# One transformer layer on one core: V in 512-column matmuls, and an opening whose VectorE and ScalarE steps stand in one fixed order

## The chip, the core and the metric

The kernel runs on one core of a Trainium2 chip. Five engines matter: TensorE (PE in the profile, with its weight loads as PEld), VectorE (DVE), ScalarE (ACT), GpSimd (POOL) and SyncE (SP, which issues most DMAs). Each engine works through its own list of instructions in the order in which they were put there, and waits at semaphores for the others. The metric is the device time of one execution in microseconds (us): 1761.19 us is the median of three runs of the kernel before (1760.97 to 1761.48).

## The reference

One decoder layer over 1024 tokens of 1024 channels in float32, cut to what matters here:

```
h = rms_norm(x, attn_norm_w)
q, k, v, u, g = split(h @ w_in)         # 1024, 1024, 1024, 2048, 2048 columns
a = diff_attention(rms_norm(q), rms_norm(k), v, ...)   # 8 heads
c = causal_depthwise_conv(u_a * sigmoid(u_b), conv_w)  # width 31
c = silu(layer_norm(c))
x = x + (sigmoid(g_a) * (a @ w_pa) + sigmoid(g_b) * (c @ w_pc)) @ w_out
x = x + (silu(h2 @ w_g) * (h2 @ w_u)) @ w_down         # h2 = rms_norm(x)
```

The change touches the first line, the V columns of `w_in`, and the order in which the first steps are done. What is computed stays the same.

## The kernel before

**Every product in three.** Each float32 operand is split into a high part (a cast on ScalarE, `split_hi`, L119) and a low part (a subtraction on VectorE, `split_lo`, L124). A product of two operands is three matmuls, high by high, high by low and low by high, added up in one PSUM bank.

**Stages.** The first stage forms h, transposed and split as `hT_hi` and `hT_lo`, and from it V (stored to DRAM), the u blocks (U0 to U7, 128 channels each, with the gated product stored to DRAM) and the first head's q and k. Then comes attention, head by head, into whose gaps the other q, k and gate columns are worked. The projections, the output product and the feed-forward part follow. On VectorE the 248 multiply-adds of the convolution ("taps", L519 and L525, on 128x1024 tiles) run as a background list from the first u block to the end of attention; a fixed rate of 3.25 taps per item step is handed out in the first stage (`TAPS_FIRST`).

**The opening.** x comes in eight tiles of 128 tokens (`xt`). For each, ScalarE squares and sums it (L609), VectorE and ScalarE form the reciprocal root (L573 to L578, L603), VectorE multiplies two halves by it and by the norm's weights (L613, `xt<-xt,r,anw_b`), PE transposes eight 128x128 pieces into two PSUM tiles (L616, `px`, two buffers), ScalarE casts them to `hT_hi` and VectorE subtracts to `hT_lo`. The norm's weights are read from DRAM once for every partition (L173, 512 KB into `anw_b`).

**V and u.** V is four items of 256 columns (V0 to V3). An item's weights are two tiles of 128x1024 (`ld_wide`), and for every token tile 24 matmuls run with a 128x128 block of hT as the stationary operand and 256 weight columns as the moving one (L152 to L154, `pg<-whi,hT_hi`). A u item is two blocks of weights, each multiplied with the two halves of the tokens: the weights stand, 512 tokens move (`pg<-hT_hi,whi`), 24 matmuls for each half and block.

**What sets the order.** A scheduler puts the instructions on each engine by its own estimate of when each would be ready, unless `after(...)` holds a piece back behind a named instruction. The list of items (`first`) sets which come early: V0, U0, U1, V1 and so on. In the kernel before, nothing holds the opening's pieces in an order, and the scheduler interleaves norms, transposes and matmuls.

## Time and profile before

| what | value |
|---|---|
| median of three runs | 1761.19 us (1760.97 to 1761.48) |
| the profiled execution's own time | 1761.41 us |
| its span, first to last instruction | 1759.6 us |
| PE busy | 1740.3 us (99%) |
| weight loads, PEld | 1503.1 us (85%) |
| VectorE busy | 1273.2 us (72%) |
| ScalarE busy | 800.5 us (45%) |
| DMA, mean | 156 GB/s |

The profiled execution lies 0.2 us above the median; 1.8 us of its time lie outside the span. A matmul's duration in the trace runs from its start to the end of its drain, and the next one starts before that: the rate is read from start to start. "Idle before" an instruction is put down to the engine or DMA whose semaphore came last.

### The profile page before, as it was taken

What the parts mean: (1) busy time and instruction counts of PE and PEld (TensorE: products, weight loads), DVE (VectorE), ACT (ScalarE), POOL (GpSimd) and SP (SyncE); (2) the same over time, 40 slices, a digit from 0 to 9 for tenths busy, and PEclk for the clock granted to TensorE, in tenths of its full rate; (3) what the DMA queues carried; (4) which work ended last, traced back from release to release, by engine and by line L of the source; (5) the groups of instructions that cost most, each with busy time, mean ns of one, the idle gap of its engine ahead of it and who ended that gap; (6) DMA issues with size and microseconds to landing.
All of it is one profiled execution on the core that took longest, in us unless ns stands there. A gap on an engine that the chain in (4) does not pass through costs nothing.

```text
span 1759.6 us, 25844 instructions
## 1 busy us (share of the span) xinstructions
PE 1740.3 (99%) x9367; PEld 1503.1 (85%) x9367; DVE 1273.2 (72%) x2187; ACT 800.5 (45%) x1886; POOL 26.7 (2%) x106
## 2 busy tenths in 40 slices
PE   7999999999999999999999999999999999999999
PEld 6898998988999998988888888888888888888887
DVE  6388879999988888886687534877667666664544
ACT  4211241558767776655557313643333333333332
POOL 3000000000000000000000000000000000000000
PEclk9999999999999999999999999999999999999999
DMA  8433353235444344352983544234544544697663
GB/s 248 164 121 114 108 158 124 76 96 151 111 138 124 88 114 138 86 163 76 336 268 108 168 167 144 91 102 146 177 150 158 176 157 139 210 360 242 215 216 131
DMA packets 255728, 275.34 MB, mean 156 GB/s; under 512 B 16064, under 2 KB 177896, under 8 KB 255600
## 3 DMA queue, kind: packets, MB, share of 16 engines
q1 hardware_dynamic: 253568, 267.45, 47.6%
q0 software_dynamic: 1744, 5.19, 1.0%
q8 instruction: 74, 1.21, 0.3%
q10 hardware_dynamic: 288, 1.05, 0.2%
q14 instruction: 54, 0.44, 0.1%
HBM read 176.59 MB, written 78.68 MB: 145 GB/s over the span
## 4 chain that ended last, share of the span: by engine, by line
PE 95%; DMA 2%; ACT 1%; DVE 1%; issue 0%; SPq 0%; ACTq 0%
PE acc L1375 22%; PE pg L153 15%; PE pg L154 15%; PE pg L152 15%; PE acc L451 12%; PE sc L817 2%; PE sc L816 2%; PE wo L154 2%; PE wo L153 2%; PE wo L152 2%; PE pT L852 2%; PE pW L152 1%; PE pW L154 1%; PE pW L153 1%; PE pQ L714 1%; DMA wraw<-in_w_in_dram 1%
## 5 line engine op out<-in xcount | busy, mean ns | idle before, releaser
L525 DVE SCALAR_TENSOR_TENSOR acc<-u,cw,acc 128x1024 f32<-128x1024 f32 x240 | 306.8, 1278 | 2.8
L152 PE MATMUL pg<-whi,hT_hi 128*128 128x256 f32 x768 | 220.3, 287 | 1.2 <-ACT hT_hi L119 1.2
L154 PE MATMUL pg<-whi,hT_lo 128*128 128x256 f32 x768 | 219.8, 286 | 0.4 <-DVE hT_lo L124 0.4
L153 PE MATMUL pg<-wlo,hT_hi 128*128 128x256 f32 x768 | 219.1, 285 | 0.2 <-DVE wlo L124 0.2
L119 ACT CAST whi<-wraw 128x1024 fp32r<-128x1024 f32 x109 | 114.4, 1051 | 215.9 <-PE pg L153 122.1
L152 PE MATMUL pg<-hT_hi,whi 128*128 128x512 f32 x512 | 201.6, 394 | 0.0
L154 PE MATMUL pg<-hT_hi,wlo 128*128 128x512 f32 x512 | 200.9, 393 | 0.0
L153 PE MATMUL pg<-hT_lo,whi 128*128 128x512 f32 x512 | 200.5, 392 | 0.0
L124 DVE TENSOR_TENSOR wlo<-wraw,whi 128x1024 fp32r<-128x1024 f32 x109 | 132.8, 1219 | 70.8 <-ACT whi L119 66.7
L124 DVE TENSOR_TENSOR wlo<-draw,whi 128x1024 fp32r<-128x1024 f32 x75 | 91.8, 1224 | 89.6 <-ACT whi L119 84.3
L152 PEld LDWEIGHTS pg<-whi,hT_hi 128*128 128x128 f32 x768 | 147.7, 192 | 4.2 <-ACT hT_hi L119 2.5
L154 PEld LDWEIGHTS pg<-whi,hT_lo 128*128 128x128 f32 x768 | 147.8, 192 | 2.3 <-DVE hT_lo L124 1.1
L153 PEld LDWEIGHTS pg<-wlo,hT_hi 128*128 128x128 f32 x768 | 147.7, 192 | 2.0 <-DVE wlo L124 0.5
L119 ACT CAST whi<-draw 128x1024 fp32r<-128x1024 f32 x75 | 79.1, 1055 | 129.5 <-PE acc L451 125.9
L451 PE MATMUL acc<-wlo,whi 128*128 128x512 f32 x308 | 119.8, 389 | 0.0
L451 PE MATMUL acc<-whi,wlo 128*128 128x512 f32 x308 | 119.8, 389 | 0.0
L823 ACT ACTIVATE E<-E,mn 128x256 f32<-128x256 f32 (+7 forms) x128 | 99.7, 779 | 35.8 <-DVE mn L818 33.6
L154 PEld LDWEIGHTS pg<-hT_hi,wlo 128*128 128x128 f32 x512 | 96.2, 188 | 19.0
L153 PEld LDWEIGHTS pg<-hT_lo,whi 128*128 128x128 f32 x512 | 96.2, 188 | 18.7
L152 PEld LDWEIGHTS pg<-hT_hi,whi 128*128 128x128 f32 x512 | 96.3, 188 | 18.3
L1375 PE MATMUL acc<-h_hi,whi 128*128 128x512 f32 x240 | 93.4, 389 | 0.0
L1375 PE MATMUL acc<-h_lo,whi 128*128 128x512 f32 x240 | 93.4, 389 | 0.0
(270 smaller groups left out, 3951.5 us busy)
## 6 DMA issues: line engine op xcount, KB each, us to landing
wraw<-in_w_gate_up_dram SPq DMA_DIRECT2D x44, 512.0 KB, 4.8
wraw<-in_w_in_dram SPq DMA_DIRECT2D x40, 512.0 KB, 4.5
qs<-qs SPq DMA_DIRECT2D x96, 128.0 KB, 2.3
wd<-in_w_down_dram SPq DMA_DIRECT2D x44, 256.0 KB, 3.1
tdT<-wd SPq DMA_DIRECT2D x88, 128.0 KB, 4.3
draw<-sdS SPq DMA_DIRECT2D x44, 256.0 KB, 3.8
draw<-tdT SPq DMA_DIRECT2D x44, 256.0 KB, 3.9
wraw<-in_w_in_dram SPq DMA_DIRECT2D x32, 256.0 KB, 3.3
```

The costliest lines, as they stand in the source:

```text
L119: act.copy(dst, src)
L124: last_lo[0] = dve.tensor_tensor(dst, src, f32(hi), op=ALU.subtract).ins
L152: pe.matmul(o, lh, rh, start=start, stop=False)
L153: pe.matmul(o, lh, rl, start=False, stop=False)
L154: last_mm[0] = pe.matmul(o, ll, rh, start=False, stop=stop).ins
L451: m = pe.matmul(o[s_][i][:], l_[:, ts], r_[:, 512:], start=start and j + y_ == 0, stop=j == n - 1 and y_ == 2, skip_group_check=not start,)
L525: dve.scalar_tensor_tensor(acc[0][:], us[c][:, t : t + S], cw[:, c, t : t + 1], acc[0][:], op0=ALU.mult, op1=ALU.add)
L816: pe.matmul(o[:, :w], qh[:, qs], k, start=True, stop=False)
L817: last_mm[0] = pe.matmul(o[:, :w], ql[:, qs], k, start=False, stop=True).ins
L823: act.activation(e[:, :nk], e[:, :nk], AF.Exp, bias=mn[:, j : j + 1], scale=-1.0, accum_out=l[:, j : j + 1])
L852: pe.transpose(pt[:, k * P : (k + 1) * P], e[:, (k0 + k) * P : (k0 + k + 1) * P], ident[:])
L1375: pe.matmul(o[:], a_[x_][:, k, :], b_[y_][:, k, :], start=start and k + x_ + y_ == 0, stop=k == 3 and x_ == 1, skip_group_check=not start,)
```

## The change

V is now two items of 512 columns. Its weights come in four tiles of two 128-row blocks each (`ld_pair`), split into tiles of their own pool (`vw`), and each token tile takes 24 matmuls with 512 moving columns. In the list of items V0's first four token tiles and U0 leave the list and go into a function `opening`; the rest of V0 stands after U2, V1 after U3.

`opening` issues the DMAs for x and V's weights in one sequence, and then makes twenty steps. Each step is held behind the last instruction that VectorE and ScalarE have been given so far, so the steps keep one order on these two engines. A step is a weight tile's high or low part, the statistics of a token tile (`stat`), or its product, transposes and split (`norm`). Behind them come the small vectors (`vectors`), V0's first four token tiles and U0. The norm's weights are read as two rows of 512 (2 KB each) and spread over the partitions by two float32 matmuls with a column of ones (`spread_weights`). The first token tile's statistics are made in two halves, one on ScalarE and one on VectorE. Fewer buffers hold x (three, not four).

```
+    def spread_weights():
+        for g in range(2):
+            pt = pm()
+            pe.matmul(pt[:], one[:], anw[g], start=True, stop=True)
+            act.copy(wb[:, 512 * g : 512 * (g + 1)], pt[:])
...
-    first = ["V0", "U0", "U1", "V1", "U2", "U3", "V2", "U4", "Q0", "V3", "U5", "U6", "U7"]
+    first = ["U1", "U2", "V0", "U3", "V1", "U4", "Q0", "U5", "U6", "U7"]
...
+    def v_item(j, tiles=None):
+        w = [v0[k] for k in range(4)] if j == 0 else [ws.next() for k in range(4)]
+        for i in tiles or range(4 if j == 0 else 0, NT):
             o = pg()
...
+            ts = slice(i * P, (i + 1) * P)
+            terms = [(k, a_, b_) for k in range(NKT) for a_, b_ in ((0, 0), (0, 1), (1, 0))]
+            if i == j == 0:
+
+                terms.sort(key=lambda t_: (t_[2], t_[1], t_[0]))
+            for n_, (k, a_, b_) in enumerate(terms):
+                l_, r_ = (hT_hi, hT_lo)[a_][:, k, ts], w[k // 2][b_][:, k % 2, :]
+                last_mm[0] = pe.matmul(o[:], l_, r_, start=n_ == 0, stop=n_ == len(terms) - 1).ins
...
+        for step in (
+            lambda: (stat(0), spread_weights()),
+            lambda: (hi(0), norm(0)),
+            lambda: lo(0),
+            lambda: (hi(1), lo(1)),
+            lambda: (hi(2), stat(1)),
+            lambda: lo(2),
+            lambda: (hi(3), norm(1)),
+            lambda: (xload(3), stat(2), lo(3)),
+            lambda: norm(2),
+            lambda: (xload(4), stat(3)),
+            lambda: norm(3),
+            lambda: (xload(5), stat(4)),
+            lambda: uw.append(ws.next()),
+            lambda: norm(4),
+            lambda: (xload(6), stat(5)),
+            lambda: norm(5),
+            lambda: (xload(7), stat(6)),
+            lambda: norm(6),
+            lambda: stat(7),
+            lambda: norm(7),
+        ):
+            with after(last_of(mybir.EngineType.DVE)), after(last_of(mybir.EngineType.Activation)):
+                step()
+        with after(last_of(mybir.EngineType.DVE)), after(last_of(mybir.EngineType.PE)):
+            vectors()
+        uw.append(ws.next())
+        ws.ahead = 2
+        yield from v_item(0, range(4))
+        yield from u_item(0, uw)
```

**PE, the first token tile.** Before, the eight transposes of the first token tile (`px`) are followed by its V matmuls, in threes (high by high, low weights, low hT), as the two weight tiles `whi_10` and `whi_13` allow:

```order
L616 MATMUL px_7_353<-ident_78,xt0_90 128x128 x4
L616 MATMUL px_8_361<-ident_78,xt0_90 128x128 x4
L152 MATMUL pg_21_398<-whi_10_370,hT_hi_334 128x256
L153 MATMUL pg_21_398<-wlo_11_371,hT_hi_334 128x256
L154 MATMUL pg_21_398<-whi_10_370,hT_lo_335 128x256
```

Now the two spreading matmuls (`pm_17`, `pm_18`) come first, and the first tile takes the high parts of all four weight tiles (`vwh_5`, `vwh_7`, `vwh_9`, `vwh_11`) before anything else:

```order
L186 MATMUL pm_17_356<-anw0_90,one_92 128x512
L186 MATMUL pm_18_359<-anw1_91,one_92 128x512
L656 MATMUL px_19_364<-ident_78,xt0_96 128x128 x4
L656 MATMUL px_20_372<-ident_78,xt0_96 128x128 x4
L675 MATMUL pg_74_636<-vwh_5_334,hT_hi_320 128x512 x2
L675 MATMUL pg_74_636<-vwh_7_336,hT_hi_320 128x512 x2
L675 MATMUL pg_74_636<-vwh_9_338,hT_hi_320 128x512 x2
L675 MATMUL pg_74_636<-vwh_11_340,hT_hi_320 128x512 x2
L675 MATMUL pg_74_636<-vwh_5_334,hT_lo_321 128x512 x2
```

What moved: the high parts of the fourth weight tile are needed after six matmuls of the first token tile, where before the second of two tiles was needed after twelve.

**PE, the transposes of the last token tiles.** Before, the transposes of tile 5 (`px_56`, `px_57`) stand between V matmuls of the token tiles before it and U0's first product (`pg_81`):

```order
L152 MATMUL pg_45_603<-whi_13_376,hT_hi_334 128x256
L153 MATMUL pg_45_603<-wlo_14_377,hT_hi_334 128x256
L154 MATMUL pg_45_603<-whi_13_376,hT_lo_335 128x256
L616 MATMUL px_56_671<-ident_78,xt5_454 128x128 x4
L616 MATMUL px_57_679<-ident_78,xt5_454 128x128 x4
L152 MATMUL pg_81_841<-hT_hi_334,whi_16_382 128x512
L153 MATMUL pg_81_841<-hT_lo_335,whi_16_382 128x512
L154 MATMUL pg_81_841<-hT_hi_334,wlo_17_383 128x512
```

Now those of the tiles 5, 6 and 7 (`xt5`, `xt6`, `xt7`) follow each other behind the last matmul of U0's first half (`pg_88`), with the transposes of the small vectors (`pm_69`, `pm_70`) behind them; the matmuls of U0's second half (`pg_89`, `pg_91`) and of U1's first (`pg_101`) come after:

```order
L155 MATMUL pg_88_787<-hT_hi_320,wlo_48_501 128x512
L656 MATMUL px_55_536<-ident_78,xt5_477 128x128 x4
L656 MATMUL px_56_544<-ident_78,xt5_477 128x128 x4
L656 MATMUL px_61_567<-ident_78,xt6_520 128x128 x4
L656 MATMUL px_62_575<-ident_78,xt6_520 128x128 x4
L656 MATMUL px_67_596<-ident_78,xt7_551 128x128 x4
L656 MATMUL px_68_604<-ident_78,xt7_551 128x128 x4
L232 MATMUL pm_69_611<-ident_78,rows_100 128x64
L240 MATMUL pm_70_617<-ident_78,cwrow_112 128x31 x8
L153 MATMUL pg_89_814<-hT_hi_320,whi_44_494 128x512
L153 MATMUL pg_91_841<-hT_hi_320,whi_47_500 128x512
L153 MATMUL pg_101_893<-hT_hi_320,whi_72_632 128x512
```

What moved: no matmul stands any more between the transposes of one of these tiles and those of the next.

**VectorE, the last token tiles.** Before, tile 7's reciprocal root (from `v_68`) and its product with x (`xt7`) stand ahead of the low parts of tile 5 (`px_56`, `px_57`); VectorE has every tile's product done before PE comes to its transposes:

```order
L603 TENSOR_SCALAR v_68_773<-ss_67_771 128x1
L124 TENSOR_TENSOR vl_44_598<-pg_30_486,vh_43_597 128x512
L124 TENSOR_TENSOR hT_lo_335<-px_51_626,hT_hi_334 128x4x128
L574 RECIPROCAL r_69_775<-t_70_776 128x1
L575 TENSOR_TENSOR t_70_776<-r_69_775 128x1
L576 SCALAR_TENSOR_TENSOR t_70_776<-v_68_773,t_70_776 128x1
L577 TENSOR_SCALAR t_70_776<-t_70_776 128x1
L578 TENSOR_TENSOR r_69_775<-r_69_775,t_70_776 128x1
L613 SCALAR_TENSOR_TENSOR xt7_571<-xt7_571,r_69_775,anw_b_92 128x512 x2
L124 TENSOR_TENSOR hT_lo_335<-px_56_671,hT_hi_334 128x4x128
L124 TENSOR_TENSOR hT_lo_335<-px_57_679,hT_hi_334 128x4x128
```

Now tile 6's root (from `v_58`) and product (`xt6`) stand behind both low parts of tile 5 (`px_55`, `px_56`), and ahead of tile 5's stands U0's gated product (`sg_87`), which needs U0's first half to be finished on PE:

```order
L653 SCALAR_TENSOR_TENSOR xt5_477<-xt5_477,r_53_527,anw_b_99 128x512 x2
L572 TENSOR_TENSOR sg_87_785<-pg_88_787,sg_87_785 128x512
L125 TENSOR_TENSOR hT_lo_321<-px_55_536,hT_hi_320 128x4x128
L125 TENSOR_TENSOR hT_lo_321<-px_56_544,hT_hi_320 128x4x128
L627 TENSOR_SCALAR v_58_556<-ss_57_554 128x1
L598 RECIPROCAL r_59_558<-t_60_559 128x1
L599 TENSOR_TENSOR t_60_559<-r_59_558 128x1
L600 SCALAR_TENSOR_TENSOR t_60_559<-v_58_556,t_60_559 128x1
L601 TENSOR_SCALAR t_60_559<-t_60_559 128x1
L602 TENSOR_TENSOR r_59_558<-r_59_558,t_60_559 128x1
L653 SCALAR_TENSOR_TENSOR xt6_520<-xt6_520,r_59_558,anw_b_99 128x512 x2
L125 TENSOR_TENSOR hT_lo_321<-px_61_567,hT_hi_320 128x4x128
```

What moved: a token tile's product now waits in VectorE's list for the low parts of the tile before it, and those wait for its transposes on PE. ScalarE's list has the same order: the square of tile 6 (`xj6`) stands behind both casts of tile 5.

More of the change, by code (lines that the diff above doesn't have):

```diff
@@ L1 @@
 import math
+from itertools import chain
 from contextlib import ExitStack, nullcontext
@@ L357, with vtiles @@
     TAPS_FIRST = 3.25
+    def vtiles():
+        return [vw.tile([P, 1024], F32R, tag=t_, name=nm(t_), bufs=4) for t_ in ("vwh", "vwl")]
     def loads_of(it):
@@ L361, in loads_of @@
         if it[0] == "V":
-            return ld_wide(win, [(V0 + 256 * c, 256)])
+            return [ld_pair(win, k, V0 + 512 * c, vtiles) for k in range(0, NKT, 2)] if c else []
         if it[0] == "Q":
@@ L367, in loads_of @@
         return ld_cols(win, G0 + c * P)
-    for it in first + [x_ for l_ in later for x_ in l_]:
+    for it in ["U0"] + first + [x_ for l_ in later for x_ in l_]:
         ws.plan(loads_of(it))
@@ L754, in run, with opening, hi, lo @@
                 yield
+    def opening():
+        raws = [wraw(), wraw()] + [ap.tile([P, 1024], F32, tag="vraw", name=nm("vraw"), bufs=2) for k in range(2)]
+        for k, raw in enumerate(raws):
+            nc.sync.dma_start(
+                raw[:].rearrange("p (k c) -> p k c", c=512),
+                win[2 * k * P : 2 * (k + 1) * P, V0 : V0 + 512].rearrange("(k p) c -> p k c", p=P),
+            )
+            if k in (1, 2):
+                xload(k)
+        wt = [vtiles() for k in range(4)]
+        def hi(k):
+            split_hi(wt[k][0][:], raws[k][:])
+        def lo(k):
+            split_lo(wt[k][1][:], raws[k][:], wt[k][0][:])
+            v0[k] = [t_[:].rearrange("p (k c) -> p k c", c=512) for t_ in wt[k]]
+        uw = []
+        for step in (
[28 more added lines that the diff above has]
+        yield from u_item(0, uw)
     n = 0
     due = 0.0
-    for _ in run(first):
+    for _ in chain(opening(), run(first)):
         n += 1
         if n == 16:
-            bias_rows()
+            with after(last_of(mybir.EngineType.DVE)):
+                bias_rows()
         if n >= 18 and n % 3 == 0 and (n - 18) // 3 < H:
```

150 lines of the change are left out of this document (76 added, 74 removed).

## The prediction, made before the changed kernel was run

> **What bounds the kernel now.** I read the page's busy shares and its chain of waits first, then the busy time by stretches, then the opening row by row.
>
> ```profile
> PE 1740.3 (99%) x9367; PEld 1503.1 (85%) x9367; DVE 1273.2 (72%) x2187; ACT 800.5 (45%) x1886; POOL 26.7 (2%) x106
> PE 95%; DMA 2%; ACT 1%; DVE 1%; issue 0%; SPq 0%; ACTq 0%
> ```
>
> TensorE is busy for 99% of the span and makes 95% of the chain that ended last. So the time is PE's work plus the places where PE stands or runs at a slow clock. The busy times by stretches (columns: length, then busy us and instructions of PE, PEld, DVE, ACT, POOL, granted clock, DMA share, GB/s) show where it stands:
>
> ```profile
> 0.00:40.00 40.00, 28.71 (x170) 24.14 (x171) 27.69 (x88) 21.60 (x43) 14.15 (x35) 1.00 0.79 235
> 40.00:80.00 40.00, 40.00 (x235) 35.45 (x234) 12.72 (x17) 11.58 (x16) 0.00 (x0) 1.00 0.63 211
> 360.00:800.00 440.00, 437.25 (x2966) 401.34 (x2966) 393.12 (x926) 304.51 (x1040) 10.42 (x58) 1.00 0.42 119
> 800.00:860.00 60.00, 59.19 (x301) 48.87 (x300) 33.14 (x63) 31.33 (x70) 0.93 (x5) 1.00 0.46 163
> ```
>
> The first 40 us hold 11.3 us of idle PE. Then PE never waits until attention, where 2.75 and 0.81 us are idle. From 40 to 80 us, the stretch whose order the change rewrites, there is nothing to win and much to lose.
>
> **Term 1: 512 columns, -5.0 us.** V has 8 token tiles x 8 k x 3 x 4 items = 768 matmuls of 256 columns; the change makes them 384 of 512. By groups up to 59.9 us (last columns: busy us, mean ns of one | idle before), and from start to start in PE's timeline (start, duration):
>
> ```profile
> L152 PE MATMUL pg<-whi,hT_hi 128*128 128x256 f32 x64 | 20.1, 314 | 1.2 <-ACT hT_hi L119 1.2
> L152 PE MATMUL pg<-hT_hi,whi 128*128 128x512 f32 x15 | 6.0, 397 | 0.0
> ```
>
> ```profile
> 40.42 0.28 PE L154 MATMUL pg<-whi,hT_lo 128*128 128x256 f32 x1
> ...
> 42.94 0.28 PE L154 MATMUL pg<-whi,hT_lo 128*128 128x256 f32 x1
> ...
> 61.14 0.39 PE L152 MATMUL pg<-hT_hi,whi 128*128 128x512 f32 x1
> ...
> 79.95 0.39 PE L154 MATMUL pg<-hT_hi,wlo 128*128 128x512 f32 x1
> ```
>
> Durations mislead: a matmul starts before the last one has drained. From 40.42 to 42.94 stand 21 intervals, 2.52/21 = 0.120 us each; from 61.14 to 79.95 stand 83, 18.81/83 = 0.2266. Two small ones cost 0.240, one large 0.2266: 13 ns a pair, x 384 = 5.0 us. The Trainium skill, "TensorE: Matmul & The Clock Gate", "Back-to-back issue gap", has a warm gap of N/2.4 + 2.5 ns, which by estimate would save 2.5 ns a pair, 1.0 us in all, and the sum below would be 1777. The trace shows 13 ns, so the trace's number stands.
>
> **Term 2: the opening up to the end of U0's first half, +1.7 us.** Rows of ACT, DVE and PE:
>
> ```profile
> 6.02 1.06 ACT L609 ACTIVATE xj<-xt 128x1024 f32<-128x1024 f32 x1 [4.00 <-DMA xt<-in_x_dram]
> 10.78 1.04 ACT L119 CAST whi<-wraw 128x1024 fp32r<-128x1024 f32 x1 [3.19 <-DMA wraw<-in_w_in_dram]
> 17.90 1.06 ACT L609 ACTIVATE xj<-xt 128x1024 f32<-128x1024 f32 x1 [0.45 <-DMA xt<-in_x_dram]
> ...
> 9.45 1.94 PE L616 MATMUL px<-ident,xt 128*128 128x128 f32 x8 [9.45 <-DVE xt L613]
> 12.37 0.58 PE L152 MATMUL pg<-whi,hT_hi 128*128 128x256 f32 x1 [0.98 <-ACT hT_hi L119]
> 18.17 0.41 PE L153 MATMUL pg<-wlo,hT_hi 128*128 128x256 f32 x1
> 18.38 0.41 PE L154 MATMUL pg<-whi,hT_lo 128*128 128x256 f32 x1
> 28.61 0.60 PE L616 MATMUL px<-ident,xt 128*128 128x128 f32 x4
> 28.97 0.36 PE L152 MATMUL pg<-whi,hT_hi 128*128 128x256 f32 x1
> 29.17 0.28 PE L153 MATMUL pg<-wlo,hT_hi 128*128 128x256 f32 x1
> 19.67 0.59 ACT L119 CAST hT_hi<-px 128x512 fp32r<-128x512 f32 x1 [0.61 <-PE px L616]
> 20.29 0.69 DVE L124 TENSOR_TENSOR hT_lo<-px,hT_hi 128x512 fp32r<-128x512 f32 x1
> ```
>
> Before: up to 60.0 us PE did 192 small matmuls (23.0 us), 43 large (9.7), 16 groups of four transposes at 29.17 - 28.61 - 0.12 = 0.44 (7.0), and the bias and small-vector matmuls, about 3.2. That is 43.0 of 60.0: 17.0 us lost, before the first transposes and at the slow rate after them.
>
> After: the fourth weight tile is the seventh 512 KB block in the queue (x0, three weight tiles and two x tiles ahead). Before, the third block (x0 and `anw_b` ahead of it) landed at 10.78, the eighth at 17.90, so 1.42 each: the seventh at 10.78 + 4 x 1.42 = 16.5, cast by 17.5. Until then only six matmuls of the first token tile can run. Its 18 others take 4.1, and 0.9 more while the rate is still slow: 22.5. Each next tile is 0.88 (transposes) + 0.85 (PE stands until cast and low part, 0.59 and 0.69, let the matmuls go) + 24 x 0.2266 = 7.2; three tiles: 44.0. U0's first half with tile 4's transposes is 48 x 0.2266 + 0.88 = 11.8: 55.8. Of it 144 x 0.2266 + 10 x 0.44 = 37.0 is work, 18.8 lost: 1.7 more than before. Bounds -1 (all eight blocks earlier, since the 512 KB of `anw_b` leave the queues) and +4 (6.2 us of slow rate counted anew from 17.5).
>
> **Term 3: the stall of tiles 5 to 7, +9.4 us.** Between the transposes of tiles 5, 6 and 7 PE now has no matmul, and each tile's square on ACT stands behind the casts of the tile before. One tile's chain is in the trace:
>
> ```profile
> 7.20 0.15 DVE L603 TENSOR_SCALAR v<-ss 128x1 f32<-128x1 f32 x1 [7.20 <-ACT xj L609]
> 8.60 1.41 DVE L613 SCALAR_TENSOR_TENSOR xt<-xt,r,anw_b 128x512 f32<-128x512 f32 x2
> 39.33 1.42 DVE L613 SCALAR_TENSOR_TENSOR xt<-xt,r,anw_b 128x512 f32<-128x512 f32 x2
> 50.48 0.60 PE L616 MATMUL px<-ident,xt 128*128 128x128 f32 x4
> 44.79 1.28 ACT L545 ACT_TABLE_LOAD   x1
> ```
>
> From the square (6.02) to the first transposes (9.45) are 3.43 us. From a tile's first transposes to the next tile's square: 0.71 (second half's product), 0.60 (its transposes), 0.59 (its cast), 1.9. A cycle is 5.3; two are 10.6, and the last tile's 1.9 and 0.3 to the first matmul make 12.8. Work in it: 3 x 0.88 + 0.8 for the small vectors = 3.4. Lost: 9.4. Before, the last tile's product was done at 40.8 and its transposes came at 50.48: ten us of lead that hid the whole chain. That lead is the cover now gone. ACT's table loads (1.28) may stand twice more around tile 5; U0's matmuls hide them, or they add 1.3 each. Late next: U0's second half, so its gated product, so the first convolution taps. Bounds: 6 (PE reaches tile 5 before its product is ready, part of it counted above) and 13.
>
> **Term 4: the slow rate again, +1.6 us.** After PE's idle start, matmuls of 256 columns went 0.21 apart (18.17 to 18.38) and later 0.120. From 12.37 to 18.6 that is 6.2 us at half rate, 3.1 lost. Term 3 holds two pauses of 5.3 - 0.88 = 4.4 us. Whether one of that length brings the slow rate back no row shows: between 0 and 3.1 I take the middle. On this the Trainium skill, same page, "HAM oscillation — how this bites in real kernels", asks for no PE idle gap over about 3.4 us; by it the pauses slow the clock, and by the trace's own 3.1 the sum would be 1774.6.
>
> **Term 5: attention, +4 us.** The order of all engines changes up to the end of attention, where DVE has 393 of 440 us and PE waits 2.75. The taps behind it:
>
> ```profile
> L525 DVE SCALAR_TENSOR_TENSOR acc<-u,cw,acc 128x1024 f32<-128x1024 f32 x240 | 306.8, 1278 | 2.8
> ```
>
> The first tap starts some ten us later, eight taps of 1.278, handed out at the same rate per step. Bounds: -3 (the idle there vanishes) and +8 (most of the backlog reaches PE); I take +4, as an engine at 89% has little room.
>
> **At nothing.** The bias broadcasts' DMAs only move later, under U's matmuls (uncovered: some 12 us of landing). V's stores carry the same bytes under V. The seventh x tile is issued late, with three buffers, and lands under U0. The small vectors are needed by the first taps only, behind tile 7. The spreading matmuls run before x's product; uncovered, 1 to 2 us.
>
> **Sum.** The profiled execution took 1761.4, 0.2 over the median. 1761.4 - 5.0 + 1.7 + 9.4 + 1.6 + 4 = 1773.1: 1773.
>
> **Rivals.** *PE does not stand* (faster): the norms of tiles 5 to 7 run under U0's first half, as before. 1761.4 - 5.0 + 1.7 = 1758. It needs 5.3 us, 23 matmuls, between one tile's transposes and the next; PE stood 0.98 at 12.37 with nothing passing it. *A bare stall*: no slow clock, attention unchanged, 1761.4 + 6.1 = 1767. *Backlog*: the full slow clock and +8, 1761.4 + 6.1 + 3.1 + 8 = 1779. *The durations are right*: 2 x 287 - 394 = 180 ns x 384 = 69 us, 1692; the start times of 83 matmuls speak against it.
>
> ```profile
> L152 PE MATMUL pg<-whi,hT_hi 128*128 128x256 f32 x768 | 220.3, 287 | 1.2 <-ACT hT_hi L119 1.2
> L152 PE MATMUL pg<-hT_hi,whi 128*128 128x512 f32 x512 | 201.6, 394 | 0.0
> ```
>
> **How the numbers follow.** Forecast 0.64, bare stall 0.16, backlog 0.11, no stall 0.07, durations 0.02. A measurement of this kernel tells 0.2%, 3.5 us, from no change. No stall gives faster by 3 and falls on both sides of that bound: with the durations, faster 0.06; the rest of it, and a bare stall at its lower bounds (term 2 and 3 each 3 less), is same, 0.08; slower 0.86. The forecast's own range is 1768 to 1779; with the rivals beside it 1763 to 1781.
>
> **What would show it.** V's 512-column matmuls start 0.2266 apart. Between 55 and 70 us PE stands twice for some 4.4 us, ahead of the transposes of tiles 6 and 7, released by DVE's product. Right behind, 0.43 to 0.45 between starts shows the slow rate. The first tap comes near 90 us. Idle PE from 360 to 860 grows from 3.6 to some 8 us. I am wrong if those pauses are under 2 us each, if a matmul stands between these transposes, or if attention loses more than the stall.

## The result, and the profile after

The changed kernel takes 1781.9 us (median; 1780.7 to 1782.69), beside 1761.08 us for the kernel before on the same chip: a ratio of 1.0119, 95% interval 1.0102 to 1.0137. Slower was forecast, by 12 us; it became 21, and the time lies 0.9 us above the stated range. Every cost came out at its term or above it, and none had another sign.

The page of the changed kernel, busy shares and chain of waits:

```profile
PE 1748.2 (98%) x8987; PEld 1486.7 (83%) x8987; DVE 1280.0 (72%) x2189; ACT 806.3 (45%) x1890; POOL 26.7 (1%) x107
PE 93%; DMA 3%; ACT 2%; DVE 1%; issue 1%; SPq 0%; ACTq 0%
```

PE's busy time rose by 8 us although it has 380 matmuls fewer. That is the first sign of a slow rate: a matmul at half rate is busy for longer. The busy times by stretches (columns as in the prediction; the stretches of attention are moved by 20 us) show where:

```profile
0.00:40.00 40.00, 30.44 (x103) 20.50 (x104) 19.68 (x46) 15.31 (x28) 9.52 (x27) 1.00 0.63 195
40.00:80.00 40.00, 30.95 (x137) 24.60 (x135) 22.69 (x56) 17.83 (x30) 0.00 (x0) 0.79 0.32 99
380.00:820.00 440.00, 431.98 (x2933) 395.90 (x2932) 386.76 (x910) 302.61 (x1031) 10.43 (x58) 1.00 0.41 118
820.00:880.00 60.00, 58.27 (x299) 48.63 (x298) 33.64 (x63) 32.30 (x73) 0.92 (x5) 1.00 0.46 159
```

From 40 to 80 us, where PE had been busy throughout, it now stands for 9 us, and the granted clock is 0.79 instead of 1.00. (The trace holds no clock record for the first 19 us of the kernel before and 24 us of the changed one, and the column shows 1.00 there; in the opening the slow rate is read from the spacing of the matmuls.) In attention it stands for 8.0 and 1.7 us instead of 2.75 and 0.81. PE's timeline (start, duration, and in brackets the idle time before it with what ended it) shows the stall:

```profile
43.66 0.39 PE L675 MATMUL pg<-vwh,hT_hi 128*128 128x512 f32 x1
...
46.15 0.39 PE L675 MATMUL pg<-vwh,hT_lo 128*128 128x512 f32 x1
...
59.63 1.34 PE L656 MATMUL px<-ident,xt 128*128 128x128 f32 x8 [0.64 <-PE pg L155]
64.92 1.94 PE L656 MATMUL px<-ident,xt 128*128 128x128 f32 x8 [3.95 <-issue]
70.80 1.94 PE L656 MATMUL px<-ident,xt 128*128 128x128 f32 x8 [3.94 <-issue]
...
73.96 1.65 PE L153 MATMUL pg<-hT_hi,whi 128*128 128x512 f32 x3
75.41 0.63 PE L154 MATMUL pg<-hT_lo,whi 128*128 128x512 f32 x1
...
78.40 0.63 PE L155 MATMUL pg<-hT_hi,wlo 128*128 128x512 f32 x1
78.82 0.46 PE L153 MATMUL pg<-hT_hi,whi 128*128 128x512 f32 x1
79.12 0.40 PE L154 MATMUL pg<-hT_lo,whi 128*128 128x512 f32 x1
```

The transposes of the tiles 5, 6 and 7 start at 59.63, 64.92 and 70.80 with two pauses of 3.95 us between them. "issue" names no releaser; ScalarE's and VectorE's rows show what fills the first pause: the casts of tile 5, then the square of tile 6, then, behind its root, the product of tile 6.

```profile
60.30 1.29 ACT L120 CAST hT_hi<-px 128x512 fp32r<-128x512 f32 x2 [2.52 <-PE px L656]
61.49 1.06 ACT L638 ACTIVATE xj<-xt 128x1024 f32<-128x1024 f32 x1
64.06 1.41 DVE L653 SCALAR_TENSOR_TENSOR xt<-xt,r,anw_b 128x512 f32<-128x512 f32 x2
```

Behind the first pause the eight transposes take 1.94 us instead of 1.34, and the matmuls from 75.41 to 78.40 stand 0.427 apart (2.99 us over 7 intervals) instead of 0.227. The granted clock falls inside the first pause: it is 1.00 in its first 0.8 us and 0.50 in the rest (columns as above).

```profile
60.97:61.80 0.83, 0.00 (x0) 0.00 (x0) 0.82 (x2) 0.80 (x2) 0.00 (x0) 1.00 0.15 62
61.95:64.92 2.97, 0.01 (x1) 0.04 (x1) 2.17 (x9) 0.89 (x3) 0.00 (x0) 0.50 0.14 53
```

V's new matmuls are 11 intervals in 2.49 us, 0.226 each, as forecast.

To compare programs with different matmuls I count **lost time**: the time passed, less the matmuls started until then, each at its full-rate spacing (0.2266 us for 512 columns, 0.120 for 256, 0.176 for 384, 0.11 for a transpose). All matmuls of a kernel so priced are its **work**. The bias matmuls, float32 and slower than this count (2.1 us), run in the opening before and near 140 us now; their 2.1 us are taken out of the opening. "Opening" is the lost time up to 100 us, "attention" that from the first score matmul to the end of the projections' sums, "taps" how many of the convolution's 240 multiply-adds behind the first of each block are done when the first score starts (within one), all from the profiled execution. The ratio is to runs of the kernel before on the same chip.

| kernel | median us | ratio, 95% interval | span | work | opening | attention | taps |
|---|---|---|---|---|---|---|---|
| before | 1761.1 | | 1759.6 | 1720.7 | 16.6 | 14.9 | 120 |
| changed | 1781.9 | 1.0119 (1.0102 to 1.0137) | 1780.9 | 1716.0 | 35.3 | 22.2 | 121 |
| 1 products ahead | 1776.8 | 1.0087 (1.0073 to 1.0100) | 1773.3 | 1716.0 | 29.3 | 20.5 | 121 |
| 2 V0 whole in the opening | 1778.0 | 1.0093 (1.0080 to 1.0106) | 1776.4 | 1716.0 | 23.6 | 28.2 | 110 |
| 3 512 columns alone | 1778.7 | 1.0097 (1.0083 to 1.0111) | 1775.9 | 1715.6 | 24.2 | 28.3 | 109 |
| 4 pauses filled | 1774.5 | 1.0073 (1.0059 to 1.0087) | 1770.1 | 1716.0 + 6.3 | 29.6 | 16.8 | 121 |
| 5 products ahead, tile 4 | 1766.5 | 1.0030 (1.0018 to 1.0041) | 1763.6 | 1716.0 | 20.4 | 18.9 | 117 |
| 6 as 3, 3.6 taps | 1770.9 | 1.0054 (1.0042 to 1.0067) | 1769.5 | 1715.6 | 26.8 | 19.6 | 114 |
| 7 changed, 3.5 taps | 1778.2 | 1.0098 (1.0083 to 1.0113) | 1779.1 | 1716.0 | 33.1 | 22.6 | 126 |
| 8 before, 3.5 taps | 1762.1 | 1.0010 (1.0001 to 1.0019) | 1760.2 | 1720.7 | 17.1 | 15.0 | 126 |
| 9 half of V wide | 1762.4 | 1.0007 (0.9998 to 1.0016) | 1760.4 | 1718.1 | 16.7 | 17.8 | 121 |
| 10 as 5, 3.5 taps | 1768.0 | 1.0036 (1.0022 to 1.0050) | 1768.8 | 1716.0 | 22.1 | 17.6 | 122 |
| 11 changed, again | 1781.0 | 1.0111 (1.0092 to 1.0129) | 1779.5 | 1716.0 | 33.8 | 22.1 | 122 |
| 12 as 9, 3.5 taps | 1763.7 | 1.0014 (1.0005 to 1.0023) | 1765.8 | 1718.1 | 17.4 | 21.2 | 125 |
| 13 list order alone | 1763.9 | 1.0015 (1.0007 to 1.0024) | 1760.1 | 1720.7 | 16.3 | 15.0 | 121 |
| 14 list order and pools | 1762.9 | 1.0008 (0.9998 to 1.0017) | 1760.5 | 1720.7 | 16.8 | 15.3 | 121 |
| 15 as 9, 12 more matmuls | 1765.0 | 1.0021 (1.0012 to 1.0029) | 1763.9 | 1718.1 + 2.7 | 17.8 | 17.4 | 121 |
| 16 as 9, 8 taps less | 1767.1 | 1.0035 (1.0023 to 1.0047) | 1765.5 | 1718.1 | 16.2 | 23.1 | 118 |
| 17 before, 8 taps less | 1768.4 | 1.0048 (1.0034 to 1.0061) | 1766.1 | 1720.7 | 16.1 | 21.7 | 118 |

(In experiment 4 the unread matmuls' 6.3 us are counted as lost in the opening, since they fill pauses. A few matmul records are missing in some traces, half a microsecond of work at most.) For the changed kernel the account closes: -4.7 of work, +18.7 in the opening, +7.3 in attention make +21.3, and the spans differ by 21.3.

### The profile page after: what moved, and what is told of

It reads as the page before. It is cut to its first block, busy times and chain, and to the rows that moved or that the text cites. A ratio compares the mean times of both kernels' runs of the same rounds, so it can differ in the third digit from the quotient of the medians.

```text
span 1780.9 us, 25087 instructions
## 1 busy us (share of the span) xinstructions
PE 1748.2 (98%) x8987; PEld 1486.7 (83%) x8987; DVE 1280.0 (72%) x2189; ACT 806.3 (45%) x1890; POOL 26.7 (1%) x107
## 4 chain that ended last, share of the span: by engine, by line
PE 93%; DMA 3%; ACT 2%; DVE 1%; issue 1%; SPq 0%; ACTq 0%
PE acc L1460 21%; PE pg L153 13%; PE pg L154 13%; PE pg L155 13%; PE acc L472 12%; PE pg L675 5%; PE sc L902 2%; PE sc L901 2%; PE wo L153 2%; PE wo L154 2%; PE wo L155 2%; PE pT L937 1%; PE pW L155 1%; PE pW L153 1%; PE pW L154 1%
## 5 line engine op out<-in xcount | busy, mean ns | idle before, releaser
L120 ACT CAST whi<-wraw 128x1024 fp32r<-128x1024 f32 x101 | 106.1, 1052 | 188.2 <-PE pg L154 102.4
L125 DVE TENSOR_TENSOR wlo<-wraw,whi 128x1024 fp32r<-128x1024 f32 x101 | 123.1, 1220 | 74.5 <-ACT whi L120 74.4
L154 PE MATMUL pg<-wlo,hT_hi 128*128 128x256 f32 x512 | 145.9, 285 | 2.5 <-DVE wlo L125 2.5
L153 PE MATMUL pg<-whi,hT_hi 128*128 128x256 f32 x512 | 146.3, 286 | 0.9 <-ACT jk L730 0.9
L155 PE MATMUL pg<-whi,hT_lo 128*128 128x256 f32 x512 | 145.5, 284 | 0.0
L155 PEld LDWEIGHTS pg<-hT_hi,wlo 128*128 128x128 f32 x512 | 96.6, 189 | 19.6
L154 PEld LDWEIGHTS pg<-wlo,hT_hi 128*128 128x128 f32 x512 | 97.7, 191 | 3.8 <-DVE wlo L125 2.7
L153 PEld LDWEIGHTS pg<-whi,hT_hi 128*128 128x128 f32 x512 | 97.6, 191 | 2.7 <-ACT jk L730 1.5
L155 PEld LDWEIGHTS pg<-whi,hT_lo 128*128 128x128 f32 x512 | 97.7, 191 | 0.8
```

The source lines that it names most:

```text
L120: act.copy(dst, src)
L125: last_lo[0] = dve.tensor_tensor(dst, src, f32(hi), op=ALU.subtract).ins
L153: pe.matmul(o, lh, rh, start=start, stop=False)
L154: pe.matmul(o, lh, rl, start=False, stop=False)
L155: last_mm[0] = pe.matmul(o, ll, rh, start=False, stop=stop).ins
```

## The experiments

**1 to 4: the stall, the columns, the slow rate.** My theory: the written order of the steps makes the stall, the pauses bring the slow rate, and 512 columns save 13 ns a pair. The rivals: PE would have waited anyway, the wide V itself costs, the slow rate has another cause.

*Experiment 1* splits `norm` into `prod` (the product) and `turn` (transposes and split) and writes the steps in another order:

```
-            lambda: norm(4),
-            lambda: (xload(6), stat(5)),
-            lambda: norm(5),
-            lambda: (xload(7), stat(6)),
-            lambda: norm(6),
-            lambda: stat(7),
-            lambda: norm(7),
+            lambda: prod(4),
+            lambda: (xload(6), stat(5)),
+            lambda: prod(5),
+            lambda: turn(4),
+            lambda: (xload(7), stat(6)),
+            lambda: prod(6),
+            lambda: stat(7),
+            lambda: prod(7),
+            lambda: turn(5), turn(6), turn(7)
```

> The changed kernel with one edit in the opening's written order: the square, root and product of the token tiles 5 to 7 stand ahead of the splits of the tiles before them; the matmuls and the V items stay. Theory (the stall costs 9.7 us and the slow rate behind it 4.3): the transposes of tiles 5 to 7 follow U0's first half without a pause over 1.5 us, the 512-column matmuls behind them stay 0.227 apart, the first tap comes near 87 us, and the time is 1781.9 - 13 = 1769. If the late first tap is what costs 7 us in attention, these go too: 1762. Rival (PE's later work would have waited anyway): 1782, with the same idle time further on.

It took 1776.8, 5 us less than the changed kernel, not 13. PE's timeline in it:

```profile
62.37 1.71 PE L672 MATMUL px<-ident,xt 128*128 128x128 f32 x8 [3.68 <-DVE hT_lo L125]
64.53 2.07 PE L672 MATMUL px<-ident,xt 128*128 128x128 f32 x8 [0.45 <-DVE hT_lo L125]
...
69.26 0.63 PE L154 MATMUL pg<-hT_lo,whi 128*128 128x512 f32 x1
69.68 0.63 PE L155 MATMUL pg<-hT_hi,wlo 128*128 128x512 f32 x1
```

One pause of 3.68 us is left, now ended by the low parts of tile 5: these stand behind the product of tile 7 on VectorE, and the two buffers for transposed tiles come free only with them. The one pause is enough for the slow rate (0.42 from 69.26 to 69.68). The opening still loses 29.3.

*Experiment 2* runs all eight token tiles of V0 in the opening, so that 24 matmuls stand between the transposes of one tile and the next:

```
-    first = ["U1", "U2", "V0", "U3", "V1", "U4", "Q0", "U5", "U6", "U7"]
+    first = ["U1", "U2", "U3", "V1", "U4", "Q0", "U5", "U6", "U7"]
-        yield from v_item(0, range(4))
+        yield from v_item(0, range(8))
```

> The changed kernel with one edit in the list of items: all eight token tiles of V0 run in the opening, ahead of U0, so that 24 matmuls stand between the transposes of the tiles 5, 6 and 7. Theory: the pauses are filled, 13 us come back, 1769, although the first tap now comes some 20 us later than with the products ahead, near 107 us. If late taps cost in attention, PE's idle time there is larger than with the products ahead, by 10 us and more, and the time is 1779 or above.

The stall is gone: the opening loses 23.6 instead of 35.3. But attention loses 28.2, and the gain is spent. The first tap comes at 105.7 and 110 taps are done at the first score instead of 121. The missing ones are met at the end of attention, by the waits of PE and by its busy time from 820 to 850 us:

```profile
PE pT L937 <- DVE rl L914: 2.9, 1, 2.9
PE sc L901 <- DVE mn L903: 2.1, 2, 1.3
```

```profile
820.00:850.00 30.00, 23.94 (x119) 18.90 (x118) 17.65 (x41) 14.17 (x42) 0.56 (x3) 0.89 0.13 44
```

PE stands for 6 of these 30 us, waiting for VectorE's softmax steps, at a mean granted clock of 0.89.

*Experiment 3* is the kernel before with V in 512 columns and no ordered opening:

```
-    first = ["V0", "U0", "U1", "V1", "U2", "U3", "V2", "U4", "Q0", "V3", "U5", "U6", "U7"]
+    first = ["V0", "U0", "U1", "U2", "U3", "V1", "U4", "Q0", "U5", "U6", "U7"]
-            return ld_wide(win, [(V0 + 256 * c, 256)])
+            return [ld_pair(win, k, V0 + 512 * c, vtiles) for k in range(0, NKT, 2)]
```

> The kernel before with V in 512 columns alone: weights in four tiles of their own pool, three buffers for x, U's and V's items in the list as before except that V has two items; norms, transposes and the opening are left to the scheduler. Theory (13 ns a pair, 384 pairs): 1761.1 - 4.9 = 1756, with 1 to 3 us lost where the first token tile waits for the fourth weight tile: 1756 to 1759. If the 7 us lost in attention come from V's 512 columns (its stores, its loads by head), PE's idle time there grows by as much: 1763 or above. If the durations counted (180 ns a pair): 1692.

1778.7: the theory's 1756 to 1759 fell, and by its time alone the rival (1763 or above) stood; experiment 6 tells whether the columns themselves cost. The work is 5 us less, as forecast, yet the opening loses 7.6 us more (the first token tile needs all four weight tiles, and PE stands another 2.6 us ahead of 61.56) and attention 13.4 more. V0 is now some 20 us longer (192 x 0.2266 = 43.5 for 192 x 0.120 = 23.0) and U0 stands behind it: first tap at 108.5, 109 taps at the first score, and the waits at the end of attention as in experiment 2.

*Experiment 4* puts 14 unread matmuls into each of the two pauses of the changed kernel:

```
-            lambda: norm(5),
+            lambda: (norm(5), held_spin(14)),
...
-            lambda: norm(6),
+            lambda: (norm(6), held_spin(14)),
```

> The changed kernel with 14 extra 512-column matmuls behind the transposes of tile 5 and 14 behind those of tile 6; nothing reads what they write. They fit into the two pauses (14 x 0.227 = 3.2 of 3.95 us). Theory (the pauses bring the slow rate): the transposes of tiles 6 and 7 take 1.0 instead of 1.9 us, the matmuls behind start 0.227 apart at once, and 4 us come back: 1778. Rival (the slow rate there has another cause, a count of time or the transposes themselves): no change, 1782, the spacing 0.43 as before.

PE's timeline:

```profile
57.95 1.34 PE L656 MATMUL px<-ident,xt 128*128 128x128 f32 x8 [0.64 <-PE pg L155]
59.04 3.45 PE L811 MATMUL pm<-vwh,hT_hi 128*128 128x512 f32 x14
63.24 1.33 PE L656 MATMUL px<-ident,xt 128*128 128x128 f32 x8 [0.74 <-issue]
68.52 1.33 PE L656 MATMUL px<-ident,xt 128*128 128x128 f32 x8 [0.73 <-PE pm L811]
70.59 0.96 PE L153 MATMUL pg<-hT_hi,whi 128*128 128x512 f32 x3
71.39 0.40 PE L154 MATMUL pg<-hT_lo,whi 128*128 128x512 f32 x1
71.62 0.39 PE L155 MATMUL pg<-hT_hi,wlo 128*128 128x512 f32 x1
```

With pauses of 0.7 us the slow rate is gone: 1.33 instead of 1.94 us for the transposes, 0.23 between the matmuls at once. The opening loses 5.7 us less, though the tiles come no sooner (63.24 - 57.95 = 5.29 us for a cycle, as in the changed kernel's first). Pauses in PE bring the slow rate; useless matmuls keep it away. The time fell by 7.5, more than these 5.7: attention lost 16.8 instead of 22.2, although nothing of it was edited. That was the first hint at what follows.

**5 to 8: what is left of the stall, and taps against order.** *Experiment 5* adds one V0 tile to experiment 1: `v_item(0, range(5))` in the opening.

> The kernel with the products ahead (first experiment), and one more token tile of V0, tile 4, in the opening: its 24 matmuls stand between the transposes of tile 5 and those of tile 6. Theory (what was left of the stall, a wait of 3.8 us for tile 6's product and the slow rate behind it, 9 us of lost time in all between 59 and 74 us, is a matter of cover alone): no pause of PE over 1.5 us between 55 and 80, spacing 0.227 throughout, some 6 us less than the first experiment: 1776.8 - 6 = 1771. Rival (the wait is paid elsewhere): 1777.

1766.5, 5 us better than expected. PE's timeline:

```profile
62.78 1.03 PE L672 MATMUL px<-ident,xt 128*128 128x128 f32 x8
64.78 1.25 PE L672 MATMUL px<-ident,xt 128*128 128x128 f32 x8 [0.97 <-DVE hT_lo L125]
```

Products ahead and 24 matmuls of cover together take the opening from 35.3 to 20.4. So the stall was a matter of the order of steps and of cover; it was not work that PE had to wait for. The 4.7 us of work saved are still less than what is lost over the kernel before: 3.8 in the opening, 4.0 in attention.

*Experiments 6, 7 and 8* hand out taps faster: `TAPS_FIRST` from 3.25 to 3.6 in experiment 3, to 3.5 in the changed kernel and in the kernel before.

> V in 512 columns alone (third experiment) with 3.6 instead of 3.25 taps handed out per item step in the first stage. Theory (the first tap came at 108 instead of 80 us, 109 instead of 120 taps were done when attention began, and the missing ones stand ahead of the last softmaxes on VectorE, where PE lost 8 us near 830): with 120 or more taps done by then, those waits go, 8 us come back: 1778.7 - 8 = 1771. Rival (the waits at the end come from the order of attention itself): 1779.

> The changed kernel with 3.5 instead of 3.25 taps per item step in the first stage. In the changed kernel as many taps were done at the first score as before (121 and 120), yet attention loses 7 us more. Theory (not the number of taps but where single instructions stand in the new order costs there, as the wait of 2.6 us for one weight tile's low part at 639): the loss in attention moves by some us one way or the other, 1778 to 1785, and that wait may go or others come. Rival (backlog): 1781.9 - 7 = 1775.

> The kernel before with 3.5 instead of 3.25 taps per item step in the first stage. If single places in the order cost, attention's lost time (14.9 us in the kernel before) moves here too, by 2 to 8 us, without any change in the opening: 1763 to 1769. If attention's loss is backlog alone, more taps early can only help: 1761 or less.

In experiment 6 the waits at the end went (PE busy for 27.8 of the 30 us; attention loses 19.6 instead of 28.3) and the time fell by 7.7, as expected of late taps, though only 114 were done at the first score, not 120; the rest was caught up 200 us into attention. So most of experiment 3's loss in attention was late taps, not the columns. In the changed kernel it is different: 126 taps instead of 121, and attention loses 22.6, as before. Late taps do not explain its 22. The wait for a weight's low part went, and one of the same size for a key tile (`sc` for `ks`, 2.5 us) came. The kernel before lost its 15 us again, against my expectation that the order would shift it.

**9 to 14: is it the order, the pools, the list, or the wide item?** *Experiment 9* makes only the second half of V wide, behind U3, and leaves the opening alone:

```
-    first = ["V0", "U0", "U1", "V1", "U2", "U3", "V2", "U4", "Q0", "V3", "U5", "U6", "U7"]
+    first = ["V0", "U0", "U1", "V1", "U2", "U3", "V2", "U4", "Q0", "U5", "U6", "U7"]
+            if c == 2:
+                return [ld_pair(win, k, V0 + 512, vtiles) for k in range(0, NKT, 2)]
```

> The kernel before with only the second half of V in one item of 512 columns (192 of the 384 pairs); V0 and V1 stay at 256 columns, so the opening, U0 and the first tap stay where they were. Theory (13 ns a pair, and what the change loses lies in the opening, the stall and attention's order): 192 x 13 ns = 2.5 us less work, the opening's lost time as before (16.6 to 17.1 us ahead of the bias matmuls), 1760.5 - 2.5 = 1758 if attention loses its 15 us, up to 1762 if its order changes for the worse. Rival (512 columns themselves bring no gain in the time): 1760.5 or above with attention's loss unchanged.

The work is 2.6 us less (192 pairs x 13.5 ns), the opening as before, and the time the same: attention loses 2.9 more. *Experiments 10 and 12* are 5 and 9 with 3.5 taps; *experiment 11* is the changed kernel once more.

> Products ahead and tile 4 of V0 in the opening (fifth experiment), with 3.5 instead of 3.25 taps per item step. There 117 taps were done at the first score (before: 120), and attention lost 18.9 us instead of 14.9. If the missing taps cost, some 125 are done, attention loses 15 and the time is 1766.5 - 4 = 1762. If it is the order, attention stays at 17 to 22: 1765 to 1769.

> The changed kernel, a second profile. If attention's 22 us of lost time belong to the program (its order), they are there again within 1 us, with the same wait for a weight tile's low part near 639; if they belong to the single execution, they move by several us. The lost time of the opening up to the transposes of tile 5 (19.0 to 21.3 us in the profiles of programs with the same beginning) and the stall of 14 us stay.

> The second half of V in 512 columns (ninth experiment), with 3.5 instead of 3.25 taps per item step: another order for attention over the same opening. There 2.6 us less matmul work was met by 2.9 us more lost in attention. If attention's loss is a matter of the order, it comes out somewhere between 15 and 22 us and the time between 1758 and 1765; at 15 this kernel beats the kernel before by 2.5 us. If the 512-column item itself adds waits in attention, it stays at 17.8 or above: 1762.

Experiment 11 decides between program and execution: 22.1 us against 22.2, with the same wait in the same place (waits of PE: total, times, longest):

```profile
PE pg L154 <- DVE wlo L125: 2.5, 1, 2.5
```

So the loss belongs to the program. Experiments 10 and 12 gave 17.6 and 21.2 us where 5 and 9 had 18.9 and 17.8, with more taps done early in both, and neither beat the kernel before. In 10 a wait of 3.68 us for a weight's low part, ahead of attention (PE starts again at 234.40), and slow matmuls behind it cost more than attention gained. In 12 the difference is not attention's: up to the last transposes of its output (`pS`) experiments 12 and 9 have lost 10.9 and 10.8 us, and only then does PE wait 2.6 us for a cast (`aTh`, ahead of 850.83), with the granted clock at 0.66 from 850 to 855 us. The execution profiled is also the slowest of eleven (1767.5; the median is 1763.7). So 12 does not show an order that costs more in attention. *Experiments 13 and 14* add to the kernel before, at 256 columns, first the other list order (V3 directly behind V2), then also the pool of V's own weights and the later place of the q and k pool.

> The kernel before, V in 256 columns throughout, with one move in the list of items: V3 directly behind V2 instead of behind Q0, as in the ninth experiment. There attention lost 17.8 us instead of 14.9. If the list order does it, attention loses some 18 here and the time is 1763; if not, it stays at 15 and the time at 1760.5.

> The thirteenth experiment, and the weights of V2 and V3 in the pool of their own (four tiles of high and of low parts), with the pool for q and k opened only when that one is closed, as in the changed kernel; still 256 columns. If the place of these pools in memory costs in attention, its loss is 2 to 7 us above that of the thirteenth; if not, the same within 1 us, and what is left between this and the ninth experiment belongs to the 512-column item itself.

15.0 and 15.3 us lost in attention: neither the list nor the pools cost there. (Their medians are 2 to 3 us above the kernel before all the same, which the profiled executions, 1760.1 and 1760.5 long, do not show; I leave that open.)

**15 to 17: given back, or another order?** What remained was that another engine sets attention's end and takes back what PE saves ahead of it. *Experiment 15* adds 12 unread matmuls to the wide item of experiment 9; *16 and 17* skip one tap in each channel block (`if t != 15`), in experiment 9 and in the kernel before.

> The ninth experiment (second half of V in 512 columns) with 12 extra 512-column matmuls in that item, which nothing reads: 2.7 us, about what the wide item saves. Theory A (something other than PE sets where attention ends, and gives back what PE saves ahead of it): attention begins 2.7 us later, loses 15 instead of 17.8, and the time is that of the ninth experiment, 1762. Theory B (the order that came out with the wide item costs 2.5 us in attention): attention loses 17 to 18 again and the time is 1762.4 + 2.7 = 1765.

> The ninth experiment without tap 15 of each of the eight channel blocks (8 of 248 multiply-adds of the convolution are left out, 10 us of VectorE). If VectorE's load sets the end of attention there, its loss falls from 17.8 to 14 or less and the time from 1762.4 to 1758 or less; if it is the place of single instructions, it moves by 2 us either way.

> The kernel before without tap 15 of each of the eight channel blocks (8 of 248 multiply-adds are left out, 10 us of VectorE), beside the sixteenth. If VectorE's load costs in attention here too, 14.9 us of loss become 12 and the time 1758; if attention's loss before is not VectorE's load, it stays at 15 and 1761.

The 2.7 us of extra matmuls were paid in full (1765.0, attention 17.4), so nothing was given back. And with 10 us less for VectorE to do, both kernels became slower, the kernel before by 8 us (1768.4, beside 1760.5 on the same chip): attention lost 21.7 instead of 14.9. The largest waits of PE there:

```profile
PE pT L853 <- DVE E L833: 3.1, 1, 3.1
PE pW L152 <- DMA vh<-v_hi: 1.9, 2, 1.6
PE sc L817 <- DMA ks<-klo: 1.3, 1, 1.3
```

About 1.5 of the 6.8 us more are a slow stretch behind the first of these waits: the granted clock is 0.83 from 820 to 830 us, and matmuls of 256 columns stand 0.21 apart from 826.0 to 828.4. VectorE's load alone cannot be what costs when less of it costs more. What is different is where each instruction stands: the scheduler sets the order of all engines by its own estimate, and an edit ahead of attention can give attention another order. Over all runs without a backlog of taps the loss there is 15 to 23 us; the kernel before stands at the low end, and edits that hardly touch its timing (8, 13, 14) stay there. Busy times over the whole of attention, of the kernel before, the changed one and experiment 9:

```profile
318.00:814.00 496.00, 493.25 (x3334) 452.61 (x3334) 444.71 (x1032) 339.26 (x1170) 11.17 (x62) 1.00 0.41 116
```

```profile
332.00:834.00 502.00, 493.98 (x3331) 452.30 (x3330) 445.84 (x1029) 340.43 (x1170) 11.17 (x62) 1.00 0.40 114
```

```profile
316.00:814.00 498.00, 493.10 (x3332) 451.86 (x3331) 444.02 (x1031) 340.48 (x1171) 11.21 (x62) 1.00 0.40 114
```

The same busy times on each engine within 2 us, and 496, 502 and 498 us: the difference is waiting between equal work. In the changed kernel most of its 7.3 us lie in one place. Between the 229th and the 265th of the 384 score matmuls it loses 7.4 us (from 4.3 to 11.7 since the first score), the kernel before 1.6 (3.7 to 5.3); the two stretches, the changed kernel's first:

```profile
626.00:677.00 51.00, 45.76 (x351) 42.87 (x350) 46.18 (x116) 37.99 (x156) 1.36 (x8) 1.00 0.38 99
610.00:656.00 46.00, 44.97 (x358) 43.59 (x357) 41.46 (x105) 36.04 (x154) 1.30 (x8) 1.00 0.41 110
```

The largest wait there is the one for the weight tile's low part. Its high part is ready at 635.5, but VectorE's list has a tap and softmax steps (`pl`, `E`) ahead of the low part:

```profile
634.47 1.06 ACT L120 CAST whi<-wraw 128x1024 fp32r<-128x1024 f32 x1
634.76 1.26 DVE L546 SCALAR_TENSOR_TENSOR acc<-u,cw,acc 128x1024 f32<-128x1024 f32 x1
636.35 1.15 DVE L917 SCALAR_TENSOR_TENSOR E<-E,rl,E 128x896 f32<-128x896 f32 x1
638.08 1.22 DVE L125 TENSOR_TENSOR wlo<-wraw,whi 128x1024 fp32r<-128x1024 f32 x1
639.36 0.39 PE L154 MATMUL pg<-wlo,hT_hi 128*128 128x256 f32 x1 [2.48 <-DVE wlo L125]
```

That is one place where an order costs; experiment 4, with 16.8 us lost in attention, has no such wait. The other waits were not traced one by one, and why the scheduler's estimate goes wrong there was not tried.

## Why the prediction was right or wrong

- **Term 1, 512 columns, -5.0: right.** V's own matmuls come to 5.1 us less, 13 ns a pair (1720.7 - 1715.6 in experiment 3; 2.6 us for half of the pairs in experiment 9); the changed kernel's 4.7 hold the two spreading matmuls as well. The reading from durations (1692) was wrong by 90 us, and the 2.5 ns a pair worked out from the Trainium skill, "TensorE: Matmul & The Clock Gate", "Back-to-back issue gap", were too little. But that the gain would reach the time as a gain did not hold in any kernel: alone (experiment 3) it came with a time 17 us longer.
- **Term 2, the opening, +1.7: under-sized, +4.7 in the profiled execution, above its upper bound of 4.** The step that failed is "Its 18 others take 4.1, and 0.9 more while the rate is still slow: 22.5". PE's timeline of the changed kernel:

```profile
15.80 1.22 PE L675 MATMUL pg<-vwh,hT_hi 128*128 128x512 f32 x2 [1.56 <-ACT vwh L120]
18.28 1.22 PE L675 MATMUL pg<-vwh,hT_hi 128*128 128x512 f32 x2 [1.26 <-ACT vwh L120]
19.30 3.62 PE L675 MATMUL pg<-vwh,hT_lo 128*128 128x512 f32 x8
22.72 2.30 PE L675 MATMUL pg<-vwl,hT_hi 128*128 128x512 f32 x6
24.86 1.03 PE L656 MATMUL px<-ident,xt 128*128 128x128 f32 x8
```

 The wait for the fourth weight tile was right (18.28; 17.5 was forecast). But the eight matmuls from 19.30 take 3.42, 0.43 each, and the six from 22.72 still 0.36 each on average: the slow rate lasted to some 24.3, not to about 19. Whether PE's standing between pairs of matmuls until 18.28 kept it slow was not tested. The first tile reached its last two matmuls, which stand among the second tile's, at 24.86, where 22.5 was forecast for its end; the next two tiles took 7.58 (with these two) and 7.29 instead of 7.2. U0's first half ended at 59.0, not 55.8. This size differs from one execution to the next: in experiments 4, 7 and 11, with the same steps up to there, the transposes of tile 5 start at 57.95, 57.81 and 58.42 instead of 59.63, so the size is 2.9 to 4.7, and only the execution profiled here lies above the bound.
- **Term 3, the stall, +9.4: right.** From tile 5's transposes to U0's second half 12.8 us were forecast; experiment 4, at full rate, shows 70.59 - 57.95 = 12.6, and a cycle of 5.29 where 5.3 was worked out. Less the 3.4 us of work that is 9.2, and with the 0.64 us of idle time ahead of tile 5, 9.9. Bounds and place were right too: square, root and product of one tile behind the casts of the one before.
- **Term 4, the slow rate, +1.6: under-sized, 4.1.** "I take the middle" was the failed step: two pauses of 3.95 us, with little but transposes between them, brought the slow rate in full. What the bound of 3.1 left out is that the transposes are slowed as well: 2.4 us are lost in the 11 matmuls from 73.96 to 78.82 (4.86 us for 2.49 of work), and 1.7 before, since 59.63 to 73.96 are 14.3 us where experiment 4 takes 12.6. The Trainium skill's rule of no gap over some 3.4 us, cited in the prediction, gave the right answer here; but the clock had fallen before the first pause was 1 us long, so the length of a single pause is not what the trace shows to decide.
- **Term 5, attention, +4: the sign right, the size 7.3 (inside its bounds), the mechanism wrong.** This is the largest miss. "The first tap starts some ten us later" came true in kind, but it is 19 us. VectorE's timeline before, and of the changed kernel:

```profile
80.51 2.61 DVE L525 SCALAR_TENSOR_TENSOR acc<-u,cw,acc 128x1024 f32<-128x1024 f32 x2
```

```profile
99.49 1.28 DVE L546 SCALAR_TENSOR_TENSOR acc<-u,cw,acc 128x1024 f32<-128x1024 f32 x1
```

 But no cost of it is seen here: attention begins 14 us later too, 121 taps were done at its first score, as before, and experiment 7, with 126, loses 22.6. Backlog is seen only where ten taps are missing (experiments 2 and 3; 6, with part of them made up, lost 8.7 less). The failed step is "most of the backlog reaches PE": the 7.3 us come with another order of instructions, 5.8 of them in the stretch shown above, 2.5 by one low part that stands behind other work in VectorE's list; my forecast had no term for it.
- **At nothing.** No run separates the bias rows, the stores, the x buffers and the small vectors; in the account nothing is left for them but 0.0 us (-4.7 + 18.7 + 7.3 = 21.3). The spreading matmuls, 0.4 us of work, show no other gain or loss: the first transposes came at 7.99 instead of 9.45, and PE then waited for weights.
- **The rivals.** "PE does not stand" fell by the two pauses. The bare stall fell with the slow rate. Of the rivals, "backlog" (1779) came nearest, for the right sum of the slow rate and by the wrong mechanism in attention. The range ended at 1781 because the terms 2, 4 and 5 were taken near the middle of their bounds and came out near the upper ends or above: 3.0, 2.5 and 3.3 us over.

## What to carry to other kernels

A chain that one tile's steps form over three engines (5.3 us here) was hidden here only as long as the next tile's part of it stood ahead of this tile's in each engine's list; when steps are written in a fixed order, write the statistics and the product one or two tiles ahead, and leave matmuls between the transposes. A pause of 4 us on PE cost more than itself here, since the matmuls behind the last one ran at half rate for 5 us more. And in a program whose order a scheduler sets, a gain of a few microseconds in one stage has to be measured against the 15 to 23 us that a later stage lost here from one order to another.

## What the runs showed of the hardware

In the changed kernel the granted clock fell to half 0.9 us into its first pause, when PE had made eight transposes and no other matmul for 2.9 us (59.0 to 61.9), and full rate was back some 5 us after 512-column matmuls began again (73.96 to 78.9). In experiment 1 the slow rate came with a pause of 3.68 us, in experiments 4 and 5 pauses of 0.7 to 1.0 us brought none there.

Shorter pauses brought it too, for one stretch of 3.4 us each: 2.23 us (experiment 16, ahead of 400.93), 2.6 us (experiment 3, ahead of 61.56, and 12, ahead of 850.83), 3.15 us (17, ahead of 823.59, with ten transposes and a wait of 0.6 us behind it); one of 2.48 us in the changed kernel (ahead of 639.36) brought none. In these traces every stretch at half clock between the first 20 us and the last 10 us of a kernel is a whole multiple of 3.41 us long (17.07 in the changed kernel, 10.24 in experiment 1, 3.41 in 17). The mean granted clock from 40 to 80 us is 0.79 in the changed kernel and 1.00 before. The Trainium skill, "TensorE: Matmul & The Clock Gate", "HAM oscillation — how this bites in real kernels", asks for no gap over about 3.4 us; the trace does not show that as a limit, since 2.2 to 3.15 us were enough.

I had not expected that 28 matmuls that nobody reads make a kernel 7 us faster, nor that taking 10 us of work from VectorE makes one 8 us slower.
